# GLA values and gates of a head as seven block products, with weight block sums formed in DRAM by the DMA engines

## The chip, the cores and the metric

The kernel runs on one core of one Trainium2 chip. The metric is device time in microseconds (us) of one execution, from first to last instruction, and lower is better. TensorE (PE) multiplies matrices, VectorE (DVE) and ScalarE (ACT) do elementwise work, GpSimd (POOL) does small elementwise work and issues some of the DMAs, and SyncE (SP) issues most of the weight loads. Each engine takes its own instructions strictly in order; an instruction that waits for a semaphore holds up everything behind it on that engine.

## The reference

Two residual mixers on a sequence of 512 tokens of width 1024, then a final norm; all in float32.

```python
h = h + ssd_mixer(rmsnorm(h, ssd_norm), ...)     # 8 groups, 4 heads each, both directions
h = h + gla_mixer(rmsnorm(h, gla_norm), ...)     # 4 heads, both directions
return rmsnorm(h, final_norm)

def gla_mixer(u, w_in, w_gate, b_gate, onorm, w_out):
    q, k, v, z, gl = split(u @ w_in, ...)        # per head: q, k 128 wide, v, z 512 wide; gl 32 wide in all
    lg = log_sigmoid(gl @ w_gate + b_gate) / 16  # log gates, both directions
    o = gla_scan(q, k, v, lg_forward) + rev(gla_scan(reversed inputs))
    o = rmsnorm(o, onorm) * silu(z)
    return o @ w_out
```

The change touches `v` and `z` of the GLA half: for one head they are `u` (512 x 1024) times two weight blocks of 1024 x 512.

## The kernel before, in words

**Weights.** All weights pass through one ordered list (`W.add`, `W.next`). A piece is 128 x 1024 numbers (512 KB). SP loads it (L65) into one of three raw buffers; ACT casts it to `whi` (L85, or L90 with a scale) and DVE forms the rest `wlo` (L86 or L91), each in one of three buffers. A product of two float32 matrices is three matmuls (L137, L138, L139: high by high, high by low, low by high), since both factors are kept as a high and a low part. Two pieces are split ahead of the one that PE uses.

**SSD half.** For groups 0 to 7 PE makes projections (`proj_tok` into `ptk`, `proj_ch` into `pch`), and the scan of the group before is taken in steps between them. Once, in `dt_part`, the cumulative log decays `cum` are made (tile name `dy`); POOL writes them to DRAM in eight small DMAs (`cumd`, L390). Then, for every group, POOL loads two broadcast copies of them (`bct`, L492: 1 MB each), ACT adds a bias to `bct` (L570) and takes its exponential (L578), and PE uses it as weights (L611). The small norms of the SSD outputs (`rs`, L263 and L264) are on POOL too.

**GLA half.** After the last SSD output projection (`proj_out_rows`, tiles `pr`) the norm (`norm_T`, with PE transposes `ptn`, L281) fills `uh` and `ul`, the high and low part of the normed input, transposed. For each head come q and k (48 matmuls into `pch`), the output projection of the head before (96 matmuls into `po`), the gate `z` (`proj_tok`, 96 matmuls into `ptk`), attention (`bd`, `pta`, `pto`), and the next head's `v` (96 matmuls into `ptk`). The log gates `lgc` of all four heads are made once, before head 0 (L758 to L776).

**What sets the order.** The kernel is traced in the order of its code; a scheduler then orders each engine's instructions by priority and by when their inputs can be there. DMAs that POOL issues are instructions in POOL's own queue, and the scheduler may put one ahead of code that was written earlier if nothing that it reads is still to be written.

Of the kernel before, what the change touches and what calls it, by code (L numbers as in the profile page):

```python
# [18 lines left out]
NT = 4  # L19
# [96 lines left out]
def build(tc, I, out):  # L116
    nc = tc.nc
    ctx = ExitStack()
    with ctx:
# [28 lines left out]
        # ---- inputs and constants  # L148
# [5 lines left out]
        nbc2 = cp.tile([P, D], F32, name="nbc2")  # L154
# [30 lines left out]
        rmb = cp.tile([P, L], F32, name="rmb")  # L185
        nc.vector.memset(rmb, 1.0)
        nc.vector.memset(rmf.rearrange("p (c l) -> p c l", l=P)[:, :, 0:1], 0.0)
        nc.vector.memset(rmb.rearrange("p (c l) -> p c l", l=P)[:, :, P - 1 : P], 0.0)
# [54 lines left out]
        tokm(w_in2, GV0)  # L243
# [5 lines left out]
        for hd in range(GH):  # L249
            chan(w_in2, GQ0 + hd * P)  # L250
            chan(w_in2, GK0 + hd * P)
            if hd:
                outw(w_out2, (hd - 1) * 512, onT)
            tokm(w_in2, GZ0 + hd * 512)
            if hd + 1 < GH:
                tokm(w_in2, GV0 + (hd + 1) * 512)
# [9 lines left out]
        def norm_T(t, nb, xn):  # L266
# [8 lines left out]
            for hf in range(2):  # L275
# [8 lines left out]
                split(uh[sl], ul[sl], v)  # L284

# [57 lines left out]
        nc.sync.dma_start(nbc2, I["gla_norm"][0].partition_broadcast(P))  # L343
# [3 lines left out]
        # ================= SSD  # L347
        with tc.tile_pool(name="sp", bufs=1, reuse_waits="tile") as sp:
            TM = {}

            def dt_part():
# [17 lines left out]
                for c in (9, 7, 5, 3):  # L369
# [14 lines left out]
                    out=cum[32:64, ::-1], data0=rmb[32:64, ::-1], data1=la[32:64, ::-1], initial=0.0,  # L384
# [9 lines left out]
                # token-major copies  # L394
# [84 lines left out]
            def scan_group(g, bcx, zs):  # L479
# [20 lines left out]
                # token-major x and B  # L500
# [13 lines left out]
                # C B^T, [s, l] for every chunk  # L514
# [171 lines left out]
            for g in range(G + 1):  # L686
# [20 lines left out]
                for _ in it:  # L707
                    pass
            n2 = [nbc2[:, i * 512 : (i + 1) * 512] for i in range(2)]

            proj_out_rows(yts1(3), lambda t, hf: None)
# [4 lines left out]
        with tc.tile_pool(name="gp", bufs=1, reuse_waits="tile") as gp:  # L716
# [7 lines left out]
            for d in range(2):  # L724
                w = gp.tile([96, 512], F32R, tag="al", name=f"wgs{d}", bufs=4)
# [10 lines left out]
            def v_part(pts):  # L736
                vs = []
                for t in range(NT):
                    vh = gp.tile([P, 512], F32R, tag="vh", name="vh", bufs=5)
                    vl = gp.tile([P, 512], F32R, tag="vl", name="vl", bufs=5)  # L740
                    split(vh, vl, pts[t])
                    vs.append((vh, vl))
                return vs

            lgc = gp.tile([P, 8, L], F32, tag="big", name="lgc")

            def gates():
                pt = proj_ch(96)
                gl = gp.tile([96, L], F32R, tag="bds", name="gl")
                nc.scalar.copy(gl, pt[0:96])  # L750
                nc.vector.tensor_tensor(out=gl[64:96], in0=pt[64:96], in1=gl[64:96].bitcast(F32), op=ALU.subtract)
                ab = []
                for i in range(8):
                    d, hd = i // 4, i % 4
                    pt = wkb("ptg")
                    nc.tensor.matmul(pt, lhsT=wgs[d][:, hd * P : (hd + 1) * P], rhs=gl, start=True, stop=True)
                    a = gp.tile([P, L], F32, tag=f"sc{i}", name=f"ab{i}")
                    nc.scalar.activation(a, pt, AF.Abs, bias=bgT[:, i : i + 1])  # L758
                    nc.vector.tensor_scalar(
                        out=lgc[:, i], in0=pt, scalar1=bgT[:, i : i + 1], scalar2=0.0, op0=ALU.add, op1=ALU.min  # L760
# [3 lines left out]
                for i in range(8):  # L764
                    nc.scalar.activation(ab[i], ab[i], AF.Ln, bias=1.0)
                for i in range(8):
                    a = ab[i]
                    nc.vector.tensor_tensor(out=a, in0=lgc[:, i], in1=a, op=ALU.subtract)
                    if i < 4:
                        nc.vector.tensor_tensor_scan(  # L770
                            out=lgc[:, i], data0=rmf, data1=a, initial=0.0, op0=ALU.mult, op1=ALU.add
                        )
                    else:
                        nc.vector.tensor_tensor_scan(
                            out=lgc[:, i, ::-1], data0=rmb[:, ::-1], data1=a[:, ::-1], initial=0.0,
                            op0=ALU.mult, op1=ALU.add,  # L776
                        )
# [11 lines left out]
            def att_part(hd, q, k):  # L789
                res = []  # L790
                q4, k4 = b4(q), b4(k)
                for d in range(2):
                    cu = b4(lgc[:, d * 4 + hd])
# [17 lines left out]
                    # between blocks  # L811
# [26 lines left out]
                bds = gp.tile([P, 4, P], F32, tag="bds", name="bds")  # L838
# [70 lines left out]
            vs = v_part(proj_tok())  # L909
            gates()  # L910
            for hd in range(GH):
                q, k = qk_part(hd)
                att = att_part(hd, q, k)
                if hd:
                    proj_out(yts2(hd - 1))
                zs = z_gate(proj_tok(), gp, 2)
                o_part(hd, att, vs, zs)
                if hd + 1 < GH:
                    vs = v_part(proj_tok())
# [60 lines left out]
```

## Time and profile before

| | us |
|---|---|
| median of 3 runs | 896.43 (894.97 to 897.2) |
| profiled execution, span | 894.9 |
| PE busy | 861.4 |
| DVE busy | 604.6 |
| ACT busy | 469.4 |
| POOL busy | 59.9 |

The profiled execution has no time of its own besides its span, which is 1.5 us under the median and 0.1 us under the lowest run. Sums below are made against the span's rows and then added to the median. In the page's rows a line such as L86 is a line of the kernel before; `out<-in` are tile names, `xN` a count. Busy time of PE is the union of overlapping matmul records: a single record of 0.39 us overlaps with the next, which starts about 0.23 us after it.

### The profile page before, as it was taken

The page shows a single profiled execution, that of the slowest core. Times are in us where ns is not written, and L with a number is a line of the kernel's source. Part 1 is how long each engine was busy: PE and PEld are TensorE (multiplying, and loading weights), DVE is VectorE, ACT ScalarE, POOL GpSimd, SP SyncE. Part 2 cuts the span into 40 slices and gives each one's busy share as a digit, 9 for nine tenths or more (in the row PEclk, how much of TensorE's full clock was granted, in tenths as well). Part 3 has the DMA queues.
Part 4 walks back from the last instruction along what each step waited for, and adds up shares of the span by engine and source line. Part 5 has one row for each costly group of instructions (what it writes and reads, how often), then busy time and mean ns, then how long its engine had stood idle before and what let it go on. Part 6 is the DMA issues. An engine that isn't in the chain of part 4 may idle for free.

```text
span 894.9 us, 11133 instructions
## 1 busy us (share of the span) xinstructions
PE 861.4 (96%) x4072; PEld 705.4 (79%) x4072; DVE 604.6 (68%) x954; ACT 469.4 (52%) x1038; POOL 59.9 (7%) x135
## 2 busy tenths in 40 slices
PE   7999899999999999999989997999999999999996
PEld 5778778888888888887777776878887888788875
DVE  6399889997779977798877558646432663347353
ACT  6339487756576565764855474535232533243243
POOL 2011010001000000000002000000000000100012
PEclk9999999999999999999999998999999999999999
DMA  7334334224243342433221222123231323123202
GB/s 252 95 97 168 94 118 160 96 99 124 81 127 122 113 124 80 127 118 118 95 94 42 80 71 71 48 71 94 73 92 48 95 71 94 47 94 95 94 1 94
DMA packets 72789, 86.77 MB, mean 97 GB/s; under 512 B 7074, under 2 KB 48254, under 8 KB 70687
## 3 DMA queue, kind: packets, MB, share of 16 engines
q1 hardware_dynamic: 70028, 68.62, 25.6%
q0 software_dynamic: 2704, 17.44, 5.4%
q8 instruction: 32, 0.52, 0.2%
q14 instruction: 23, 0.18, 0.1%
q10 hardware_dynamic: 2, 0.00, 0.0%
HBM read 83.82 MB, written 2.23 MB: 96 GB/s over the span
## 4 chain that ended last, share of the span: by engine, by line
PE 44%; DVE 3%; ACT 3%; POOL 1%; issue 1%; POOLq 0%; ACTq 0%; DVEq 0%
PE ptk L138 6%; PE ptk L139 6%; PE ptk L137 6%; PE po L137 3%; PE po L138 3%; PE po L139 3%; PE pto L139 2%; PE pto L137 2%; PE pto L138 2%; PE pch L137 2%; PE pch L139 2%; PE pch L138 2%; PE pr L137 1%; PE pr L139 1%; PE pr L138 1%; PE pta L846 1%
## 5 line engine op out<-in xcount | busy, mean ns | idle before, releaser
L86 DVE TENSOR_TENSOR wlo<-wraw,whi 128x1024 fp32r<-128x1024 f32 (+1 forms) x90 | 109.1, 1213 | 122.6 <-ACT whi L85 122.4
L85 ACT CAST whi<-wraw 128x1024 fp32r<-128x1024 f32 (+1 forms) x90 | 93.7, 1042 | 172.2 <-PE ptk L139 90.5
L138 PE MATMUL ptk<-wlo,uh 128*128 128x512 f32 x384 | 153.1, 399 | 4.4 <-DVE wlo L86 4.4
L137 PE MATMUL ptk<-whi,uh 128*128 128x512 f32 x384 | 152.1, 398 | 0.9 <-ACT q L785 0.8
L139 PE MATMUL ptk<-whi,ul 128*128 128x512 f32 x384 | 152.4, 398 | 0.0
L138 PE MATMUL pch<-ul,whi 128*128 128x512 f32 (+2 forms) x336 | 133.4, 397 | 0.0
L137 PE MATMUL pch<-uh,whi 128*128 128x512 f32 (+2 forms) x336 | 133.2, 396 | 0.0
L139 PE MATMUL pch<-uh,wlo 128*128 128x512 f32 (+2 forms) x336 | 131.9, 393 | 0.0
L138 PEld LDWEIGHTS ptk<-wlo,uh 128*128 128x128 f32 x384 | 73.1, 190 | 19.7 <-DVE wlo L86 5.1
L137 PEld LDWEIGHTS ptk<-whi,uh 128*128 128x128 f32 x384 | 72.9, 190 | 16.3 <-ACT q L785 1.2
L139 PEld LDWEIGHTS ptk<-whi,ul 128*128 128x128 f32 x384 | 73.2, 191 | 15.0
L137 PEld LDWEIGHTS pch<-uh,whi 128*128 128x128 f32 (+2 forms) x336 | 62.5, 186 | 13.9
L138 PEld LDWEIGHTS pch<-ul,whi 128*128 128x128 f32 (+2 forms) x336 | 62.5, 186 | 13.7 <-issue 0.3
L139 PEld LDWEIGHTS pch<-uh,wlo 128*128 128x128 f32 (+2 forms) x336 | 62.5, 186 | 13.6
L447 DVE SCALAR_TENSOR_TENSOR cv<-pch,colA,cv 128x511 f32<-128x511 f32 (+1 forms) x96 | 70.7, 742 | 0.4
L90 ACT ACTIVATE whi<-wraw,colB 128x512 fp32r<-128x512 f32 x58 | 39.3, 717 | 49.1 <-PE pch L138 35.0
L91 DVE SCALAR_TENSOR_TENSOR wlo<-wraw,colB,whi 128x512 fp32r<-128x512 f32 x58 | 41.8, 748 | 30.9 <-ACT whi L90 30.6
L570 ACT ACTIVATE bct<-bct,eb 128x128 f32<-128x128 f32 x128 | 41.1, 393 | 21.1 <-DMA bct<-cumd 21.0
L578 ACT ACTIVATE bct<-bct,eb 128x128 f32<-128x128 f32 x128 | 41.2, 392 | 7.9 <-DVE bct L575 7.9
L139 PE MATMUL po<-whi,gyl 128*128 128x512 f32 x96 | 38.5, 401 | 0.0
L137 PE MATMUL po<-whi,yh 128*128 128x512 f32 x96 | 38.1, 400 | 0.3 <-DVE h L319 0.2
L139 PE MATMUL po<-whi,yl 128*128 128x512 f32 x96 | 38.1, 396 | 0.0
(252 smaller groups left out, 1542.3 us busy)
## 6 DMA issues: line engine op xcount, KB each, us to landing
wraw<-in_ssd_w_in_dram SPq DMA_DIRECT2D x48, 512.0 KB, 4.3
wraw<-in_gla_w_in_dram SPq DMA_DIRECT2D x40, 512.0 KB, 3.7
bct<-cumd POOLq DMA_DIRECT2D x16, 1024.0 KB, 5.2
wraw<-in_ssd_w_out_dram SPq DMA_DIRECT2D x16, 512.0 KB, 3.5
wraw<-in_gla_w_out_dram SPq DMA_DIRECT2D x16, 512.0 KB, 3.6
h<-in_x_dram SPq DMA_DIRECT2D x4, 512.0 KB, 5.4
out_dram<-o SPq DMA_DIRECT2D x8, 256.0 KB, 2.0
nbc<-in_gla_norm_dram SPq DMA_DIRECT2D x1, 512.0 KB
```

The lines of the kernel that those rows point to most:

```text
L85: nc.scalar.copy(vh, raw)
L86: nc.vector.tensor_tensor(out=vl, in0=raw, in1=vh.bitcast(F32), op=ALU.subtract)
L90: nc.scalar.mul(hs[j], raw[:, j], g)
L91: nc.vector.scalar_tensor_tensor(out=ls[j], in0=raw[:, j], scalar=g, in1=hs[j].bitcast(F32), op0=ALU.mult, op1=ALU.subtract)
L137: nc.tensor.matmul(pt, lhsT=a[0], rhs=b[0], start=first, stop=False)
L138: nc.tensor.matmul(pt, lhsT=a[0], rhs=b[1], start=False, stop=False)
L139: nc.tensor.matmul(pt, lhsT=a[1], rhs=b[0], start=False, stop=last)
L447: nc.vector.scalar_tensor_tensor(out=cv[:, o0:o1], in0=pt[:, o0 + s : o1 + s], scalar=cwt(j, a), in1=cv[:, o0:o1], op0=ALU.mult, op1=ALU.add,)
L570: nc.scalar.activation(bct[:, r], bct[:, r], AF.Identity, bias=TM["eb"][:, cc, i : i + 1])
L578: nc.scalar.activation(et[:, r], et[:, r], AF.Exp, bias=TM["eb"][:, cc, i : i + 1])
L846: mm = lambda a, bb, l, r: nc.tensor.matmul(pt[:, a * P : bb * P], lhsT=l, rhs=r, start=True, stop=True)
```

## The change

`v` and `z` of a head are one product of a 2 x 2 block matrix (the normed input, blocks a11 to a22 of 256 tokens by 512 inputs) with a 2 x 2 block matrix of weights (b11 and b21 for `v`, b12 and b22 for `z`, each 512 x 512). It was 8 block products (192 matmuls in all, 8 weight pieces); it is 7 (168 matmuls, 14 weight pieces of which each now serves 12 matmuls and not 24). Four of the seven take sums of weight blocks (w1 to w4). These are formed in DRAM, per head by four copies and four accumulating DMAs of 1 MB each, issued from POOL; the code asks for one of these 32 DMAs at each scan step of the SSD half from group 1 on. Four others take sums of input blocks (s2, s3, s4, q5), formed once on DVE and split on ACT and DVE. The results are put together by 14 DVE adds per head. The log gates are made per head, and `nbc2`, the row of GLA norm weights, is loaded at the start of the GLA half. The DMA descriptor space is cut from its default to 4096 bytes per partition.

```diff
-        for hd in range(GH):
+        class Blocks:
+            def __init__(self, hd):
+                v, z = GV0 + hd * 512, GZ0 + hd * 512
+                self.b11, self.b12 = w_in2[0:512, v : v + 512], w_in2[0:512, z : z + 512]
+                self.b21, self.b22 = w_in2[512:1024, v : v + 512], w_in2[512:1024, z : z + 512]
...
+            def step(self, n):
+                w = self.w
+                cp_, ad = (lambda d, s: nc.gpsimd.dma_start(d, s)), (
+                    lambda d, s: nc.gpsimd.dma_start(d, s, accum_op=ALU.add)
+                )
+                return (
+                    lambda: cp_(w["w1"], self.b11),
+                    lambda: cp_(w["w3"], self.b12),
+                    lambda: ad(w["w1"], self.b12),
+                    lambda: ad(w["w3"], self.b22),
+                    lambda: cp_(w["w2"], w["w1"]),
+                    lambda: ad(w["w2"], self.b22),
+                    lambda: cp_(w["w4"], w["w2"]),
+                    lambda: ad(w["w4"], self.b21),
+                )[n]()
...
+                for src in (self.b11, self.b21, w["w2"], w["w1"], w["w3"], w["w4"], self.b22):
+                    for kk in range(2):
+                        W.add(src[kk * 256 : (kk + 1) * 256].rearrange("(k p) f -> p k f", p=P), (2, 512))
+
+        blocks = [Blocks(hd) for hd in range(GH)]
+        sums = [(b, n) for n in range(8) for b in blocks]
...
                 def step():
+                    if g and sums:
+                        b, i = sums.pop(0)
+                        b.step(i)
                     n = -(-left[0] // max(left[1], 1))
...
+            nbc2 = gp.tile([P, D], F32, tag="lgc", name="nbc2")
+            nc.gpsimd.dma_start(nbc2, I["gla_norm"][0].partition_broadcast(P))
+            uf = [gp.tile([P, 4, L], F32, tag=tg, name=f"uf{tg}") for tg in ("gyh", "gyl")]
             for t in range(NT):
-                norm_T(t, n2, sp.tile([P, D], F32, tag="xt", name=f"xn2{t}", bufs=2))
+                norm_T(t, n2, gp.tile([P, D], F32, tag="zs", name=f"xn2{t}", bufs=2), uf)
...
+                two = range(2)
+                p1 = block_mm("a11")
+                m1 = [keep(i, "m1") for i in two]
+                for i in two:
+                    nc.scalar.copy(m1[i], p1[i])
+                p2 = block_mm("a12")
+                for i in two:
+                    split(*vs[i], add(tmp(), p2[i], m1[i]))
+                p6 = block_mm("s2")
+                u2 = [add(keep(i, "u2"), p6[i], m1[i]) for i in two]
+                p5 = block_mm("q5")
+                p7 = block_mm("s3")
+                u3 = [add(keep(i, "u3"), p7[i], u2[i]) for i in two]
+                for i in two:
+                    gate(2 + i, p5[i], u3[i])
+                for i in two:
+                    add(u2[i], p5[i], u2[i])
+                p4 = block_mm("a22")
+                for i in two:
+                    split(*vs[2 + i], add(tmp(), p4[i], u3[i]))
+                p3 = block_mm("s4")
+                for i in two:
+                    gate(i, p3[i], u2[i])
+                return vs, zs
...
-            vs = v_part(proj_tok())
-            gates()
+            gate_low()
+            qk = qk_part(0)
+            lgc = gates(0)
+            sums_of_u()
             for hd in range(GH):
-                q, k = qk_part(hd)
-                att = att_part(hd, q, k)
+                vs, zs = vz_part()
+                att = att_part(lgc, *qk)
                 if hd:
                     proj_out(yts2(hd - 1))
-                zs = z_gate(proj_tok(), gp, 2)
+                if hd + 1 < GH:
+                    qk = qk_part(hd + 1)
+                    lgc = gates(hd + 1)
                 o_part(hd, att, vs, zs)
...
-    nc = bacc.Bacc("TRN2", target_bir_lowering=False, num_devices=1)
+    nc = bacc.Bacc("TRN2", target_bir_lowering=False, num_devices=1, dynamic_dma_scratch_size=4096)
```

**Order on POOL, between the first norm and the first scan, before.** `n` and `nhalf` belong to the norm, `cumd` is the store of the log decays, `bct` the two broadcast loads of group 0; the names in brackets are the semaphores that an instruction waits for (DMASW0 to DMASW7: POOL's DMAs by turns).

```order
L274 TENSOR_TENSOR n_196<-n_196,nhalf 128x1 [waits Pool_49]
L390 DMA cumd<-dy 8x4x128 [waits DVE_49]
L390 DMA cumd<-dy 8x4x128
L390 DMA cumd<-dy 8x4x128 [waits DVE_49]
L390 DMA cumd<-dy 8x4x128 x5
L492 DMA bct<-cumd 128x2048 [waits DMASW2_49,DMASW3_49,DMASW1_49,DMASW0_49]
L492 DMA bct<-cumd 128x2048 [waits DMASW6_49,DMASW7_49,DMASW5_49,DMASW4_49]
```

The same place of the changed kernel; `wsumw` is a block of weight sums (L256 copies, L257 adds).

```order
L257 DMA wsumw_2_109<-in_gla_w_in_dram 512x512 [waits DMASW2_49]
L257 DMA wsumw_3_113<-in_gla_w_in_dram 512x512 [waits DMASW3_49]
L424 DMA cumd<-dy 8x4x128 [waits DVE_49]
L424 DMA cumd<-dy 8x4x128
L424 DMA cumd<-dy 8x4x128 [waits DVE_49]
L424 DMA cumd<-dy 8x4x128
L424 DMA cumd<-dy 8x4x128 [waits DMASW4_49]
L424 DMA cumd<-dy 8x4x128 [waits DMASW5_49]
L424 DMA cumd<-dy 8x4x128 [waits DMASW6_49]
L424 DMA cumd<-dy 8x4x128 [waits DMASW7_49]
L526 DMA bct<-cumd 128x2048 [waits DMASW2_49,DMASW3_49,DMASW1_49,DMASW0_49]
L526 DMA bct<-cumd 128x2048 [waits DMASW6_49,DMASW7_49,DMASW5_49,DMASW4_49]
```

All 32 DMAs of the weight sums have moved ahead of the `cumd` store: the first stands among POOL's set-up instructions, before the first norm, and the two adds shown here are the last. A DMA that reads a block or adds to it waits for the DMA that wrote the block, and the last four `cumd` stores wait for the last four adds.

**Order on ACT, where the first `bct` is used, before.** `whi` is a weight piece cast for PE, `cv` and `th` belong to the projections of group 1.

```order
L443 ACTIVATE cv_670<-pch,colB,colA 128x512 [waits PE_49]
L570 ACTIVATE bct<-bct,eb 128x128 [waits DMASW0_49]
L570 ACTIVATE bct<-bct,eb 128x128 x5
L513 COPY bt_696<-ptb 128x512 [waits PE_49]
L570 ACTIVATE bct<-bct,eb 128x128 x2
L570 ACTIVATE bct<-bct,eb 128x128 [waits DMASW1_49]
L85 CAST whi_851<-wraw_849 128x1024 [waits DMAHW4_49,PE_49]
```

And in the changed kernel:

```order
L477 ACTIVATE cv_681<-pch,colB,colA 128x512 [waits PE_49]
L604 ACTIVATE bct<-bct,eb 128x128 [waits DMASW0_49]
L604 ACTIVATE bct<-bct,eb 128x128 x5
L547 COPY bt_708<-ptb 128x512 [waits PE_49]
L604 ACTIVATE bct<-bct,eb 128x128 x2
L604 ACTIVATE bct<-bct,eb 128x128 [waits DMASW1_49]
L85 CAST whi_864<-wraw_862 128x1024 [waits DMAHW3_49,PE_49]
```

Nothing has moved here: the next weight piece is cast behind the first nine uses of `bct`, as before.

**Order on PE, at the end of the SSD half, before.** `ptk` is the first `v` projection, token block by token block; `ptn` the transposes of the norm.

```order
L138 MATMUL ptk_4415<-wlo_4170,uh 128x512
L281 MATMUL ptn<-idn,xn_4337 128x128 x4
L139 MATMUL ptk_4415<-whi_4169,ul 128x512
L281 MATMUL ptn<-idn,xn_4337 128x128 x4
L137 MATMUL ptk_4417<-whi_4163,uh 128x512
L281 MATMUL ptn<-idn,xn_4363 128x128 x4
L138 MATMUL ptk_4417<-wlo_4164,uh 128x512
```

And in the changed kernel, where `pr` is the last SSD output projection and `pch` the low-rank gate input:

```order
L137 MATMUL pr_4316<-xchw_4197,yh_3921 128x512
L138 MATMUL pr_4316<-bchw_4199,yh_3921 128x512
L139 MATMUL pr_4316<-xchw_4197,yl_3922 128x512
L314 MATMUL ptn<-idn,xn_4338 128x128 x8
L314 MATMUL ptn<-idn,xn_4366 128x128 x8
L314 MATMUL ptn<-idn,xn_4394 128x128 x8
L314 MATMUL ptn<-idn,xn_4422 128x128 x8
L137 MATMUL pch<-uh,whi_4208 96x512
```

The projections that stood between the transposes are gone from there: PE now goes through all four token blocks of the norm before the first product, which reads all 512 tokens at once.

## Rows read from the trace of the kernel before

**Rows 1.** The page's first part: busy time and share of the span, by engine.

```profile
PE 861.4 (96%) x4072; PEld 705.4 (79%) x4072; DVE 604.6 (68%) x954; ACT 469.4 (52%) x1038; POOL 59.9 (7%) x135
```

**Rows 2.** Timeline of POOL: start us, us, engine, line, op [idle before <-releaser].

```profile
64.31 4.67 POOL L390 DMA_DIRECT2D cumd<-dy  x8 [52.31 <-DVE dy L380]
68.98 0.59 POOL L492 DMA_DIRECT2D bct<-cumd  x1
70.75 0.57 POOL L492 DMA_DIRECT2D bct<-cumd  x1 [1.18 <-DMA cumd<-dy]
```

**Rows 3.** Timeline of ACT around the first use of bct.

```profile
75.75 1.87 ACT L570 ACTIVATE bct<-bct,eb 128x128 f32<-128x128 f32 x6 [0.23 <-DMA bct<-cumd]
...
79.30 1.05 ACT L85 CAST whi<-wraw 128x1024 fp32r<-128x1024 f32 x1
```

**Rows 4.** Busy time by stretch up to that use (DMA share, GB/s last).

```profile
0.00:22.40 22.40, 16.92 (x71) 12.04 (x72) 15.09 (x26) 14.03 (x32) 5.03 (x20) 1.00 0.74 252
22.40:44.80 22.40, 22.40 (x100) 17.21 (x99) 8.23 (x10) 8.46 (x12) 0.00 (x0) 1.00 0.35 95
44.80:67.20 22.40, 21.86 (x101) 17.48 (x100) 21.59 (x29) 8.48 (x12) 2.88 (x5) 1.00 0.35 97
67.20:75.80 8.60, 8.60 (x38) 6.62 (x37) 8.38 (x15) 7.44 (x16) 2.93 (x6) 1.00 0.72 263
```

**Rows 5.** DMA queues of the page: packets, MB, share of 16 engines' span.

```profile
q1 hardware_dynamic: 70028, 68.62, 25.6%
q0 software_dynamic: 2704, 17.44, 5.4%
...
HBM read 83.82 MB, written 2.23 MB: 96 GB/s over the span
```

**Rows 6.** DMA issues: count, KB each, median us to landing.

```profile
bct<-cumd POOLq DMA_DIRECT2D x16, 1024.0 KB, 5.2
```

**Rows 7.** Timeline of PE in the first GLA head: a wait and the matmuls around it.

```profile
542.78 0.39 PE L137 MATMUL ptk<-whi,uh 128*128 128x512 f32 x1
543.01 0.39 PE L138 MATMUL ptk<-wlo,uh 128*128 128x512 f32 x1
...
548.77 0.80 PE L138 MATMUL ptk<-wlo,uh 128*128 128x512 f32 x1 [4.24 <-DVE wlo L86]
549.37 0.63 PE L139 MATMUL ptk<-whi,ul 128*128 128x512 f32 x1
...
554.49 0.48 PE L138 MATMUL ptk<-wlo,uh 128*128 128x512 f32 x1
```

**Rows 8.** Timeline of PE at the end of the SSD half: last pr, transposes.

```profile
486.04 0.39 PE L139 MATMUL pr<-xchw,yl 128*128 128x512 f32 x1
...
491.48 0.63 PE L281 MATMUL ptn<-idn,xn 128*128 128x128 f32 x4 [0.73 <-DVE xn L276]
...
495.10 0.60 PE L281 MATMUL ptn<-idn,xn 128*128 128x128 f32 x4
```

**Rows 9.** Timeline of DVE there: the last part of the normed input.

```profile
496.35 0.69 DVE L143 TENSOR_TENSOR ul<-ptn,uh 128x512 fp32r<-128x512 f32 x1
```

**Rows 10.** Busy time in 90 us of the GLA half (columns as in Rows 4).

```profile
590.00:680.00 90.00, 89.25 (x412) 73.14 (x410) 43.29 (x64) 33.35 (x57) 2.96 (x8) 1.00 0.26 77
```

**Rows 11.** Groups of DVE by line, GLA half: count, busy us, mean ns.

```profile
L86 DVE TENSOR_TENSOR wlo<-wraw,whi 128x1024 fp32r<-128x1024 f32 x9 | 11.0, 1225 | 27.1 <-ACT whi L85 27.1
L91 DVE SCALAR_TENSOR_TENSOR wlo<-wraw,colB,whi 128x512 fp32r<-128x512 f32 x8 | 5.7, 749 | 6.2 <-ACT whi L90 6.2
L319 DVE TENSOR_TENSOR h<-h,po 128x512 f32<-128x512 f32 x8 | 5.2, 682 | 1.2 <-PE po L139 1.2
```

**Rows 12.** Groups of DVE by line, where the log gates are made.

```profile
L759 DVE TENSOR_SCALAR lgc<-ptg,colB 128x512 f32<-128x512 f32 x8 | 5.6, 746 | 2.9 <-ACT ab L758 2.9
L768 DVE TENSOR_TENSOR ab<-lgc,ab 128x512 f32<-128x512 f32 x8 | 5.1, 682 | 2.1 <-ACT ab L765 2.1
L770 DVE TENSOR_TENSOR_SCAN lgc<-rmf,ab 128x512 f32<-128x512 f32 x4 | 4.7, 1211 | 0.0
```

More of the change, by code (lines that the diff above doesn't have):

```diff
@@ L284, in norm_T @@
                 split(uh[sl], ul[sl], v)
+                if uf is not None:
+                    nc.scalar.copy(uf[hf][:, :, t * P : (t + 1) * P], v)
         def proj_ch(m=P):
@@ L712, in build, with blk @@
             for t in range(NT):
-                norm_T(t, n2, sp.tile([P, D], F32, tag="xt", name=f"xn2{t}", bufs=2))
-        with tc.tile_pool(name="gp", bufs=1, reuse_waits="tile") as gp:
+                norm_T(t, n2, gp.tile([P, D], F32, tag="zs", name=f"xn2{t}", bufs=2), uf)
+            f1, f2 = slice(0, 256), slice(256, 512)
+            a11, a12, a21, a22 = uf[0][:, :, f1], uf[1][:, :, f1], uf[0][:, :, f2], uf[1][:, :, f2]
+            def blk(n):
+                return [gp.tile([P, 4, 256], F32R, name=f"{n}{x}") for x in "hl"]
@@ new lines, in build, with sums_of_u, sub @@
+            SB = {n: blk(n) for n in ("q5", "s2", "s3", "s4")}
+            def sums_of_u():
+                def sub(out, neg, b):
+                    nc.vector.scalar_tensor_tensor(out=out, in0=neg, scalar=-1.0, in1=b, op0=ALU.mult, op1=ALU.subtract)
+                x, y = (gp.tile([P, 4, 256], F32, tag="zs", name=f"t{n}", bufs=2) for n in ("x", "y"))
+                nc.vector.tensor_tensor(out=x, in0=a22, in1=a21, op=ALU.subtract)
+                sub(y, x, a11)
+                split(*SB["s2"], y)
+                split(*SB["q5"], x)
+                nc.vector.tensor_tensor(out=x, in0=a11, in1=a21, op=ALU.subtract)
+                split(*SB["s3"], x)
+                sub(y, y, a12)
+                split(*SB["s4"], y)
@@ new lines, in build, with block_mm @@
+            UB = {
+                "a11": (uh[:, 0:4, f1], ul[:, 0:4, f1]),
+                "a12": (uh[:, 4:8, f1], ul[:, 4:8, f1]),
+                "a22": (uh[:, 4:8, f2], ul[:, 4:8, f2]),
+                **SB,
+            }
+            def block_mm(name):
+                pts = [mmb(f"pb{i}") for i in range(2)]
+                bh, bl = UB[name]
+                for kk in range(2):
+                    wh, wl = W.next()
+                    for i in range(2):
+                        sl = slice(i * P, (i + 1) * P)
+                        for j in range(2):
+                            k = 2 * kk + j
+                            mm3(pts[i], (bh[:, k, sl], bl[:, k, sl]), (wh[j], wl[j]), k == 0, k == 3)
+                return pts
@@ L763, in gates @@
                     ab.append(a)
[L764 to L777, printed above, removed]
+                for a in ab:
+                    nc.scalar.activation(a, a, AF.Ln, bias=1.0)
+                for d, a in enumerate(ab):
+                    nc.vector.tensor_tensor(out=a, in0=lgc[:, d], in1=a, op=ALU.subtract)
+                    lv, av = (lgc[:, d], a) if d == 0 else (lgc[:, d, ::-1], a[:, ::-1])
+                    nc.vector.tensor_tensor_scan(
+                        out=lv, data0=rmf, data1=av, initial=0.0, op0=ALU.mult, op1=ALU.add
+                    )
+                return lgc
             def b4(t):
@@ L956, in build @@
                 W.alt[len(W.specs) - 1] = lambda: [
-                    [gp.tile([P, 512], F32R, tag=tg, name=f"{tg}w{j}", bufs=5) for j in range(2)] for tg in ("vh", "vl")
+                    [gp.tile([P, 512], F32R, tag=tg, name=f"{tg}w{j}", bufs=4) for j in range(2)] for tg in ("vh", "vl")
                 ]
```

82 lines of the change are left out of this document (46 added, 36 removed).

## The prediction

> **What bounds the kernel now.** I read the page's busy times first: PE is busy 861 of 895 us, DVE 605, POOL 60 [rows 1]. So PE's time is what counts, and a change pays if it takes matmuls from PE and lets no other engine make PE wait. Full-speed matmuls start 0.23 us apart [rows 7], and that is PE's price for one. Then I read the timelines where the order of the changed kernel differs, because POOL, nearly idle, is where new instructions went. The reader should see two things there. POOL stores the log decays at 64.31 us, as soon as DVE has them, and issues the first two broadcast loads at 68.98 and 70.75 us [rows 2]. ACT takes up the first of them at 75.75 us, having waited for that DMA, and casts the next weight piece for PE at 79.30 us, behind it in its queue [rows 3]. So there is a chain: POOL's queue, then `bct`, then ACT's queue, then PE's weights.
>
> **The change part by part.**
>
> *Matmuls.* 24 of 192 go per head, 96 in all: 96 x 0.23 = 22 us off PE [rows 7]. This is the whole gain.
>
> *The 32 weight-sum DMAs.* They stand in POOL's queue ahead of the `cumd` stores and so ahead of every `bct` load. POOL is in order, and the sums depend on each other, so POOL sits in front of the last adds until the earlier sums have landed. The last four `cumd` stores wait for the very last adds. So the first scan begins only when all 32 MB have been formed. Until then ACT stands at its first `bct`, the cast behind it is not made, and PE runs out of weights about 10 us later. The sum needs t, the time when the last add has landed.
>
> Price of a copy (1.05 MB from DRAM to DRAM): the trace has no such transfer; it wrote 2.23 MB in all [rows 5]. The SP queue took 25.6% of 16 engines' 894.9 us for 68.62 MB, so with all 16 engines at work 3.34 us per MB or 3.5 us for a block; POOL's queue took 5.4% for 17.44 MB, 2.9 us for a block [rows 5]. A 1 MB `bct` load lands 5.2 us after its issue [rows 6], which is the price of a lone one with its latency. Ends: 2.9 and 5.2. I take 4.4, midway between 3.5 (rows of the same kind, 2 KB and shorter pieces) and 5.2, since the destination has to be written in DRAM too. It cannot be free, because no stretch moves more than 263 GB/s [rows 4].
>
> The page "DMA: Bandwidth & Descriptors" of the Trainium skill, section "Latency and other measured facts", gives 207 to 214 GB/s for copies within DRAM in pieces of 16 KiB; no row here shows one. By it a block would take 5.0 us (an estimate), and with adds at twice that the sums would take 240 us and the kernel about 1094 us.
>
> Price of an add: the destination is read as well, so two reads for one write. Ends: the cheapest copy (2.9, the second read wholly hidden) and three passes of the dearest (15.6). I take twice the copy, 8.8. The page "Collectives: The Full Stack" of the Trainium skill, section "The bandwidth ceiling: the fold count and why AG ≠ RS ≠ AR", says that an add in the DMA engines costs its second source read and not the arithmetic; it measured a ratio of 1.93, and no row here shows it. By it the sums would take 206 us and the kernel 1061 us.
>
> Sum: 16 copies x 4.4 + 16 adds x 8.8 = 211 us of all engines. Beside them run the loads of the first 75.8 us: 0.74 x 22.4 + 0.35 x 22.4 + 0.35 x 22.4 + 0.72 x 8.6 = 38 us of all engines [rows 4], less 6 for two `bct` loads, which in the new order come later: 32 to 33. POOL issues the first copy at about 1 us. So t = 1 + 33 + 211 = 245 us.
>
> From t to the first use of `bct`: one `cumd` issue (4.67 / 8 = 0.6 us) and then the same way as before, from 68.98 to 75.75, 6.8 us [rows 2, 3]. ACT's first `bct` moves from 75.75 to 252, by 177 us. Before, the next weight piece was ready at 79.30 + 1.05 + 1.22 = 81.6 [rows 3, 11] while PE still had one of 24 matmuls (5.5 us) in hand; I take 2 us of that as slack that is used up first: 175 us. Whatever the sums do to the first 75 us (x and weights land later, POOL's small norm instructions stand between DMA issues) lies inside this wait and costs nothing, as long as it is under 170 us.
>
> After a long wait PE starts slowly. The one long wait in the trace (4.24 us) is followed by 13 matmuls in the 5.7 us from 548.77 to 554.49, about 0.43 us apart, the lower of the two clock levels, where 13 x 0.23 = 3.0 would do: 2.7 us [rows 7]. I add it once.
>
> *The norm before the GLA half.* Before, PE did projections between the transposes; now it does all transposes first and then a product that needs all tokens. From the end of the last `pr` (486.43) to the end of the last `ul` (497.04) are 10.6 us [rows 8, 9]; of these the 26 transposes left there take 3.7 (at most 0.16 us each, four in 0.63), and PE has nothing else to do now: 7 us. `nbc2`, loaded late, waits for scan work that ends before the last projection, so its landing (5.2 us for twice the bytes [rows 6]) is hidden by that projection; if it were not, up to 5 us more.
>
> *Product stage.* The fifth product's two PSUM banks are held until the sixth (s3) and two adds are done, and the next product (a22) takes the banks of s3 after the first add: 0.68 us [rows 11] and the handing over, about 1 us, and the product after it waits on a similar add. I take 1.5 us per head, 6 in all; ends 0 and 4 x 4.2 = 17, the long wait of [rows 7] once per head.
>
> *DVE and ACT.* Per head DVE gets 6 more splits (7.4 us), 14 adds (9.5) and, for heads 1 to 3, its gates (2 x (0.75 + 0.68 + 1.21) = 5.3) [rows 11, 12]: 22 us on top of 43 in 90 [rows 10], so 65 in about 85. ACT has 33 in 90 [rows 10] and gets less than that. Both stay under PE on the mean, so I cost them at nothing; what hides them is PE's own matmuls. Within the product stage it is tight: 168 x 0.23 = 39 us of PE against 14 x 1.23 + 14 x 0.68 + 4 x 0.69 + 4 x 0.75 = 32 us of DVE without attention's share. That is a rival.
>
> *The rest* (one memset fewer, descriptor space, tile places): nothing, a few tenths either way.
>
> Sum: 175 + 3 - 22 + 7 + 6 = +169. Against the span 894.9 + 169 = 1064; on the median of the runs 1065 us.
>
> **The rivals.**
> 1. *DVE sets the pace in the product stage.* For it: 32 of 39 us of DVE there before attention's instructions come in, and each piece now lasts PE 12 matmuls, 2.8 us, and not 5.5. Against: two pieces are split ahead. Price: a wait with its slow stretch as in [rows 7], 4.24 + 2.7 = 6.9 us, once per head, 28 us: 1093 us.
> 2. *The sums are cheap.* If a second read costs nothing and a copy 2.9 us, they take 32 x 2.9 = 93, t = 127, and the kernel 1065 - 118 = 947 us. For it: POOL's queue did move a block in that much engine time [rows 5]. Against: those loads do not write DRAM.
> 3. *The adds are dear.* Copies at 5.2 and adds at 15.6: 333 us, t = 367, 1187 us. For it: nothing in the trace adds in a DMA. Against: the arithmetic alone has no row that makes it slow.
> 4. *The other side: faster.* If the sums had landed when `cum` is ready at 64.31 us [rows 2], POOL's queue would hold up nothing, and the change would give -22 + 7 + 6: 887 us. It decides at t = 64: 32 x 1.05 = 33.6 MB within 63 us beside the loads, 533 GB/s, counted once; the fastest stretch moves 263 [rows 4]. A later t costs t - 70, so it would be faster up to t = 76 and within 0.3% up to 82.
>
> That the change does not do what it says is part of the forecast: the sums do not run during the SSD half, they run before its first scan.
>
> **How the numbers follow.** Forecast 0.60 (985 to 1130 us: the sums between 131 and 276 us, GLA as summed); rival 1 0.15; rival 2 0.10; rival 3 0.12; rival 4 0.03, of which 0.02 faster and 0.01 no change. I predict 1065 us. The range takes in the forecast and rival 1 and part of the way to rivals 2 and 3: 985 to 1165, about 0.78. A difference of 0.3%, 2.7 us, is about what a measurement of this kernel can tell from none. Faster 0.02, the same 0.01, slower 0.97.
>
> **What would show it right or wrong.** In the profile of the changed kernel, PE's busy tenths should fall to nothing in the slices from about 90 us to about 250 us, the DMA row be high from the start until then, ACT's longest wait be for `bct` and end where the last `cumd` store has landed, and PE's matmul records be 96 fewer with a busy total about 20 us lower. POOL should be seen waiting for its own DMAs. After the gap the SSD half should take as long as before. It is wrong if the first `bct` is used near 76 us (POOL not blocked), if PE idles in the GLA half for more than some 20 us, or if PE is fed in spite of the blocked scan.

## The result, and the profile of the changed kernel

The changed kernel takes 981.95 us (median of 4 runs, 977.90 to 985.65) against 896.82 for the kernel before (4 runs): ratio 1.0949, 95% interval 1.0914 to 1.0984, so it is slower by 85 us. The prediction said 1065 with a range of 985 to 1165. The sign and the place of the loss were right; the time lies 83 us under the forecast and just below the range.

The page of the changed kernel: busy times, then PE's row, clock and DMA row in 40 slices, and the queues.

```profile
span 983.9 us, 11252 instructions
...
PE 859.3 (87%) x3976; PEld 699.9 (71%) x3976; DVE 674.3 (69%) x1040; ACT 513.4 (52%) x1088; POOL 90.1 (9%) x168
...
PE   3937226889999999999998987999999999999997
...
PEclk9968558999999999999999997999999999999999
DMA  9999999235324243243423410362353244316302
...
q1 hardware_dynamic: 76412, 80.68, 27.8%
q0 software_dynamic: 13728, 51.52, 19.2%
...
HBM read 129.96 MB, written 35.78 MB: 168 GB/s over the span
```

PE has 96 matmuls fewer than in [rows 1], yet it is hardly less busy, since the granted clock fell in the first 170 us, to 5 tenths in two slices (1.2 GHz, the lower of its two levels), where it had stood waiting for weights. The hole is at the front: PE is at 3 tenths from 49 to 74 us and at 2 from 98 to 148 us (a slice is 24.6 us), with the DMA row full until some 165 us. From there on PE's row is at 8 or 9 almost throughout.

POOL's timeline (start us, us; in brackets the idle time before and what ended it), to lay beside [rows 2]:

```profile
114.32 0.52 POOL L256 DMA_DIRECT2D wsumw<-wsumw  x1 [4.70 <-DMA wsumw<-in_gla_w_in_dram]
120.55 0.49 POOL L256 DMA_DIRECT2D wsumw<-wsumw  x1 [5.71 <-DMA wsumw<-in_gla_w_in_dram]
126.79 0.49 POOL L256 DMA_DIRECT2D wsumw<-wsumw  x1 [5.76 <-DMA wsumw<-in_gla_w_in_dram]
130.11 1.05 POOL L257 DMA_DIRECT2D wsumw<-in_gla_w_in_dram  x1 [2.83 <-DMA wsumw<-wsumw]
133.17 1.02 POOL L257 DMA_DIRECT2D wsumw<-in_gla_w_in_dram  x1 [2.00 <-DMA wsumw<-wsumw]
136.15 1.00 POOL L257 DMA_DIRECT2D wsumw<-in_gla_w_in_dram  x1 [1.96 <-DMA wsumw<-wsumw]
...
150.39 3.48 POOL L424 DMA_DIRECT2D cumd<-dy  x6 [3.73 <-DVE dy L414]
158.11 0.54 POOL L424 DMA_DIRECT2D cumd<-dy  x1 [4.25 <-DMA wsumw<-in_gla_w_in_dram]
164.57 0.55 POOL L424 DMA_DIRECT2D cumd<-dy  x1 [5.92 <-DMA wsumw<-in_gla_w_in_dram]
165.56 0.58 POOL L526 DMA_DIRECT2D bct<-cumd  x1 [0.45 <-DMA cumd<-dy]
```

These rows give both prices. The copies of the w4 chain are released one by one as the adds before them land, 6.2 us apart; the adds after them as the copies land, 3.0 us apart. So, with the weight loads running beside them, an add costs 6.2 us and a copy 3.0. The last `cumd` store waits until 164.57 for the last add: that is t, predicted as 245. But look at 150.39: POOL had nothing left to issue before that store and waited 3.73 us for DVE to deliver the decays themselves (`dy`), which were ready at 64.31 in [rows 2].

ACT's first use of `bct`, which answers to [rows 3], and what ACT waited for in the first 171 us (total, times, longest):

```profile
170.72 1.87 ACT L604 ACTIVATE bct<-bct,eb 128x128 f32<-128x128 f32 x6 [2.26 <-DMA bct<-cumd]
```

```profile
ACT whi L85 <- DMA wraw<-in_ssd_w_in_dram: 117.0, 13, 21.4
ACT uh L142 <- PE ptn L314: 6.2, 3, 4.6
ACT xn L303 <- DMA h<-in_x_dram: 5.6, 3, 2.0
ACT bct L604 <- DMA bct<-cumd: 2.3, 1, 2.3
```

ACT hardly stood at `bct`. In all it stood 117 us waiting for weight pieces that had not come. The span grew by 89.0 us: 95.0 before the first `bct` (75.75 to 170.72), and 6.0 were won after it.

Why the weights were late, in a stretch that is all sums and weights (30 to 72 us; queue: packets, MB, share of 16 engines):

```profile
DMA packets 6917, 9.69 MB, mean 231 GB/s; under 512 B 1332, under 2 KB 3320, under 8 KB 6916
...
q0 software_dynamic: 3458, 7.85, 88.8%
q1 hardware_dynamic: 3458, 1.82, 21.0%
```

Both queues moved exactly 3458 packets. POOL's are 2.3 KB on average, those of the channel weights on SP's queue 0.53 KB, so the weights got 1.82 MB where [rows 4] show 95 GB/s (4.0 MB in 42 us). The page "DMA: Bandwidth & Descriptors" of the Trainium skill, section "Queues, rings and completion order", says that an engine takes its queues in turn, one packet at a time. These equal counts agree, if the profile's packet is the page's, which no run here shows; the experiments test the turns.

### The profile page after: what moved, and what is told of

Its sections match the earlier page's. It is cut to its first block, busy times and chain, and to the rows that moved or that the text cites. A ratio compares the mean times of both kernels' runs of the same rounds, so it can differ in the third digit from the quotient of the medians.

```text
span 983.9 us, 11252 instructions
## 1 busy us (share of the span) xinstructions
PE 859.3 (87%) x3976; PEld 699.9 (71%) x3976; DVE 674.3 (69%) x1040; ACT 513.4 (52%) x1088; POOL 90.1 (9%) x168
## 5 line engine op out<-in xcount | busy, mean ns | idle before, releaser
L86 DVE TENSOR_TENSOR wlo<-wraw,whi 128x1024 fp32r<-128x1024 f32 (+1 forms) x114 | 138.4, 1215 | 162.5 <-ACT whi L85 162.4
L85 ACT CAST whi<-wraw 128x1024 fp32r<-128x1024 f32 (+1 forms) x114 | 118.8, 1042 | 240.4 <-DMA wraw<-in_ssd_w_in_dram 117.0
L137 PE MATMUL pch<-uh,whi 128*128 128x512 f32 (+2 forms) x336 | 139.1, 415 | 38.7 <-ACT whi L85 18.8
L137 PE MATMUL ptk<-whi,uh 128*128 128x512 f32 x128 | 52.4, 409 | 9.1 <-ACT uh L142 9.1
L139 PE MATMUL ptk<-whi,ul 128*128 128x512 f32 x128 | 52.0, 406 | 0.0
L138 PE MATMUL ptk<-wlo,uh 128*128 128x512 f32 x128 | 51.5, 402 | 0.0
L296 POOL TENSOR_SCALAR rs<-ss 128x2 f32<-128x2 f32 (+1 forms) x32 | 8.3, 260 | 424.8 <-ACT gy L1010 322.7
L137 PE MATMUL pb<-whi,uh 128*128 128x512 f32 x96 | 37.8, 394 | 1.2 <-ACT whi L85 1.2
L138 PE MATMUL po<-wlo,yh 128*128 128x512 f32 x96 | 38.3, 399 | 0.0
L138 PE MATMUL pb<-wlo,uh 128*128 128x512 f32 x96 | 38.0, 395 | 0.0
```

What stands on the lines that cost most here:

```text
L85: nc.scalar.copy(vh, raw)
L86: nc.vector.tensor_tensor(out=vl, in0=raw, in1=vh.bitcast(F32), op=ALU.subtract)
L137: nc.tensor.matmul(pt, lhsT=a[0], rhs=b[0], start=first, stop=False)
L138: nc.tensor.matmul(pt, lhsT=a[0], rhs=b[1], start=False, stop=False)
L139: nc.tensor.matmul(pt, lhsT=a[1], rhs=b[0], start=False, stop=last)
L296: nc.gpsimd.tensor_scalar(out=dst, in0=ss, scalar1=mul, scalar2=add, op0=ALU.mult, op1=ALU.add)
```

## The experiments

Theory when they began: the loss lies wholly at the front and comes from the sums' transfers, which starve the weight loads there; POOL's blocked queue adds little. Rivals: the blocked queue alone; the product stage; bytes wherever they go. The table's times are medians; "SSD end" is the start of the SSD half's last `pr` matmul in the one profiled run, "rest" the span after it, so a difference of a few us in these two columns may be that run's alone (e9's six runs spread over 4.5 us). Of the kernel before they are 486.0 and 408.9 us, of the changed kernel 587.4 and 396.5.

| run | us | ratio to before (95%) | SSD end | rest |
|---|---|---|---|---|
| e1_spread | 934.48 | 1.0424 (1.0385 to 1.0464) | 533.2 | 393.7 |
| e2_nosum | 883.30 | 0.9840 (0.9815 to 0.9864) | 486.4 | 396.3 |
| e3_copies | 962.84 | 1.0725 (1.0691 to 1.0759) | 567.7 | 396.3 |
| e4_cumsp | 980.44 | 1.0916 (1.0889 to 1.0942) | 582.7 | 396.4 |
| e5_strips | 994.20 | 1.1086 (1.1034 to 1.1137) | 599.1 | 395.4 |
| e6_spread_sp | 897.63 | 1.0015 (0.9994 to 1.0037) | 498.6 | 395.2 |
| e7_late | 911.01 | 1.0156 (1.0129 to 1.0183) | 489.5 | 420.2 |
| e8_start | 904.12 | 1.0098 (1.0063 to 1.0133) | 490.2 | 412.1 |
| e9_even | 886.01 | 0.9866 (0.9836 to 0.9896) | 496.8 | 391.2 |
| e10_even1k | 887.32 | 0.9886 (0.9861 to 0.9912) | 495.1 | 390.9 |
| e11_best | 887.72 | 0.9888 (0.9864 to 0.9912) | 495.0 | 390.9 |
| e12_free | 897.96 | 1.0017 (1.0000 to 1.0035) | 507.2 | 390.6 |

**e2_nosum: what the change is worth without its sums.**

```
-    for src in (self.b11, self.b21, w["w2"], w["w1"], w["w3"], w["w4"], self.b22):
+    for src in (self.b11, self.b21, self.b22, self.b12, self.b12, self.b21, self.b22):
-sums = [(b, n) for n in range(8) for b in blocks]
+sums = []
```

> Leaves the 32 sum transfers out; the products that should read w1 to w4 read plain blocks of the weight in their place, so it is the time of everything but the sums. Theory (the sums' transfers are the whole loss): 882 to 892, middle 887, first bct near 76 us. Rival A (the product stage costs the time): 970 to 985. Rival C (the norm at the boundary, which now takes 17 us from the last output product to the first GLA product where it took 10.6, eats the gain): 893 to 900.

883.30 us. The product stage does pay: the rest of the span after the SSD half is 12.6 us shorter than before, and the SSD half as long as before. Rivals A and C fall.

**e4_cumsp: free POOL's queue, leave the sums.**

```
-    nc.gpsimd.dma_start(cumd[...], cum[...])
+    nc.sync.dma_start(cumd[...], cum[...])
-    nc.gpsimd.dma_start(bct..., TM["cumd"]...)
+    (nc.sync if g < 2 else nc.gpsimd).dma_start(bct..., TM["cumd"]...)
```

> The cumd stores and the bct loads of groups 0 and 1 are issued by SP in place of POOL, so nothing that the first scans need stands behind the sums on POOL; the sums' transfers stay as they are. Theory (weight loads starved beside the sums make cum itself late, at 150 us, so the queue adds only what lies from there to 165.6): total 955 to 975, middle 967. Rival E (the blocked queue is the loss, as the prediction had it, and the first 75 us are free): first bct near 80 to 90 us, total 895 to 910.

980.44 us: nothing won, where the predicted mechanism should have given everything back, so rival E falls. The decays are as late as in the changed kernel (the second scan that makes them starts at 150.37 us, 150.12 there). It also missed the theory's 955 to 975: the stores took SP 13 us to issue, so the `bct` loads went out at 167.22, no earlier than POOL's 165.56.

```profile
153.74 13.24 SPq L424 DMA_DIRECT2D cumd<-dy  x8
167.22 1.33 SPq L526 DMA_DIRECT2D bct<-cumd  x2
```

**e3_copies: cheap adds.** The adds become plain copies.

```
-    lambda d, s: nc.gpsimd.dma_start(d, s, accum_op=ALU.add)
+    lambda d, s: nc.gpsimd.dma_start(d, s)
```

> The 16 accumulating transfers become plain copies of the same bytes in the same places of POOL's queue (the block sums are then wrong). Theory (transfer time sets t, a copy of 1 MB takes 3.0 us and an add 6.2): t falls from 164.6 to some 16 x 3.2 = 51 us less, 113, total 925 to 940, middle 931. Rival D (the order on POOL and the waits of the adds for their copies set t, not the price of an add): 965 to 985.

962.84 us, outside the ranges of both theory and rival, but it teaches: the last sum was issued at 114.12 us, near the expected 113, but the decays came only at 144.7 us, so the saving was 19 us and not 51. POOL had issued all its sums 30 us before, and its first `cumd` store waited for DVE alone:

```profile
144.94 1.79 POOL L424 DMA_DIRECT2D cumd<-dy  x3 [30.20 <-DVE dy L414]
```

In 30 to 72 us the sums' packets are now 4.7 KB, and the weights got still less, 1.46 MB in almost exactly as many packets as the sums:

```profile
q0 software_dynamic: 2761, 13.04, 91.8%
q1 hardware_dynamic: 2764, 1.46, 13.1%
```

Faster sums starve the weights harder while they last. This run shows the starved weights as a cause by themselves: with no sum left for POOL to issue, the SSD half still ends 81 us after that of e2.

**e5_strips: shorter packets for the sums.** On top of e4:

```
+    def strips(d, s, **kw):
+        for c in range(0, 512, 128):
+            nc.gpsimd.dma_start(d[:, c : c + 128], s[:, c : c + 128], **kw)
-    cp_, ad = (lambda d, s: nc.gpsimd.dma_start(d, s)), (...)
+    cp_, ad = strips, lambda d, s: strips(d, s, accum_op=ALU.add)
```

> As e4 (the first scans need nothing from POOL's queue), but each sum goes in four strips of 128 columns, so that its packets are 512 B as those of the channel weights, at the same total of bytes. Theory F (the two busy queues take turns packet by packet, so the small packets of the weights lose against packets four times as long): in 30 to 72 us q1 moves more than twice its 1.82 MB, the cumd stores go out before 120 us in place of 150, and the total falls to 930 to 960. Rival G (what is shared is the bytes that the memory gives, whatever the packets): q1 gets no more than 2 MB there, cumd at 150 us or later, total 975 or more, since 512 B packets are no cheaper for the sums.

The mechanism came out as theory F has it, the total did not. In 30 to 72 us:

```profile
q0 software_dynamic: 6838, 6.66, 81.3%
q1 hardware_dynamic: 7895, 4.04, 35.9%
```

The weights get 4.04 MB, as much as without sums (4.09 in e1, which has none there yet), and the decays are ready at 71.5 us. The sums' packets came out at 0.97 KB on average, not 512 B. The sums moved 15% less than before in that time, far too little to explain 2.2 times the weights; so packet length decides the sharing. But the total rose to 994.20 us, because now the other cover lies bare (a cover is here a wait that hides another one of like length): the small root of each group's norm stands on POOL behind the sums, and ACT waits for it. In strips the sums also hold POOL longer: the last one was issued at 216.06 us, against 145.63 in the changed kernel.

```profile
218.15 0.91 ACT L664 ACTIVATE y<-y,rs 128x256 f32<-128x256 f32 x2 [97.84 <-POOL rs L299]
```

**e12_free: both covers gone, sums still at the front.** On top of e5:

```
-    (nc.sync if g < 2 else nc.gpsimd).dma_start(bct...)
+    nc.sync.dma_start(bct...)
-    nc.gpsimd.tensor_scalar(out=dst, ...); nc.gpsimd.tensor_tensor(out=dst, ..., op=ALU.pow)
+    nc.vector.tensor_scalar(out=dst, ...); nc.vector.tensor_tensor(out=dst, ..., op=ALU.mult)
```

> As e5 (sums at the front in strips with 512 B packets, cumd on SP), but nothing of the SSD half is left behind them on POOL: all bct loads are on SP, and the small root of each group's norm runs on VectorE, as a product in place of the power, so the norm's values are not the reference's. e5 had cum at 70 us and then lost 98 us where y waited for that root behind the sums. Theory (two covers, each as dear by itself: starved weight loads, and POOL's blocked queue; only with both gone does the front cost little): 895 to 925, the sums done near 200 us and no single wait over 15 us. Rival J (sums at the front cost their transfer time in any case): 960 or more.

897.96 us, 96 less than e5, with the same bytes moved from the first us on. The last sum was issued at 238.05, later than the 200 expected. Rival J falls: the SSD half ends 21 us after that of e2, not 100. (The roots of the GLA heads moved to VectorE too, and no kernel without sums was run in that form, so the 21 us are not exact.) So most of the loss is not the transfers but what waits for them, either in the DMA engines or in POOL's queue, and each of the two alone makes most or all of it: the starved weights 81 us in e3, the blocked queue 113 us in e5, where the strips hold it longer.

**e1_spread: the sums really in the SSD half.** POOL keeps the written order there:

```
+    with tc.manual_schedule(engines={mybir.EngineType.Pool}):
         for g in range(G + 1):
```

> The same 32 block-sum transfers, but POOL keeps the written order in the SSD loop: the first copy stands behind the cumd stores, the sums stand one by one between the bct loads of groups 0 to 5, and no sum is issued in the first 75 us. Theory (the whole loss lies at the front, where the sums starve the weight loads and hold cumd and bct): the first bct is used near 76 us as in the kernel before, the product stage keeps its gain of some 6 us, total 885 to 900, middle 891. Rival A (the product stage itself, with more VectorE work and waits, costs the time wherever the sums stand): 970 to 985. Rival B (33.5 MB of sums beside the SSD half's weights slow it wherever they stand, the first bct early but the scans late): 915 to 960, with ACT and PE waits for wraw spread over 75 to 400 us.

934.48 us. The first `bct` is back at 79.7 us, but rival B's 915 to 960 holds: the SSD half ends 47 us after that of e2, and what is waited for is `bct`, not weights as rival B had it:

```profile
ACT bct L604 <- DMA bct<-cumd: 50.2, 8, 17.6
```

In e2 ACT waits 21.3 us for `bct` and in the kernel before 21.0, so 29 us of these are new; and now they reach PE, which waits 27.9 us for the copies to `xt` that stand behind them on ACT (none in e2). A `bct` load now lands 10.6 us after its issue, where [rows 6] have 5.2.

**e6_spread_sp: the same, `bct` loads on SP's queue.**

```
-    nc.gpsimd.dma_start(bct..., TM["cumd"]...)
+    nc.sync.dma_start(bct..., TM["cumd"]...)
```

> As e1 (the sums behind the cumd stores, spread over groups 0 to 5), but the bct loads are issued by SP, so that they don't wait in the software queue behind the sums. In e1 ACT waited 50.2 us for bct. Theory H (the 43 us that e1 lacks to the 883 of the kernel without sums are bct loads standing behind sums in one queue): 885 to 900, ACT's wait for bct below 15 us. Rival I (the sums beside the other transfers slow each load whatever its queue): 915 to 935.

897.63 us, ACT's wait for `bct` 13.5 us, a landing 5.1 us. Theory H holds: in POOL's queue a load waits behind the sums issued before it; in SP's it does not. This wins 37 us. It does not win everything: the SSD half still ends 12 us after that of e2, and ACT now waits 15.0 us for weight pieces there.

**e7_late and e8_start.** e7 issues the sums of heads 2 and 3 in the GLA half; e8 also takes head 0's first two products ahead of the projections.

```
+    if hd and hd + 1 < GH:
+        for n in range(8):
+            blocks[hd + 1].step(n)
     vs, zs = vz_part()
```

> As e6, but only the sums of heads 0 and 1 (16 transfers) go in the SSD half, two for each group; those of heads 2 and 3 go at the start of heads 1 and 2 of the GLA half, POOL in written order there too. Theory H and I both: less than or the same as e6; by H 884 to 895 (the sums cost nothing once no load stands behind them), by I about half of e6's excess over 883 is gone.

911.01 us: both expectations wrong. The SSD half gets better by 9 us, but the GLA half loses 25 us against e6. There ACT waits 33.0 us for weight pieces made by the sums (1.8 in e6) and PE 13.1 us for an add on DVE:

```profile
ACT whi L85 <- DMA wraw<-wsumw: 33.0, 11, 5.3
```

These loads were not late for want of their sums. In 600 to 635 us they fetch head 1's sums, the last of which was issued at about 433 us, while head 2's are being formed; yet half of them land 10.6 us or more after their issue (count, KB each, median us to landing), where e6 has 3.5 in the same stretch:

```profile
wraw<-wsumw SPq DMA_DIRECT2D x5, 512.0 KB, 10.6
```

The two queues again move nearly equal counts there, 1837 packets of the sums and 1904 of SP's loads. So the loads are late because they share the engines with the next head's sums.

```
+    vz = vz_parts(); next(vz)        # products a11, a12 of head 0
     gate_low()
     qk = qk_part(0)
```

> As e7, and the first two products of head 0 (a11, a12: token tiles 0 and 1 alone) go ahead of the gate, query and key projections, to fill TensorE's waits at the norm between the halves, where e2 waits 9.6 us for xn. If those waits are what the norm costs: 4 to 9 us less than e7; if the products only take the place of the projections that wait for tiles 2 and 3 anyway: the same as e7 within 2 us.

904.12 us, 6.9 less than e7, as the first expectation had it; the rest after the SSD half is 8 us shorter. Between e6 and e11 below, which also differ in this start, the rest shrinks by only 4.3 us, so 8 is not what it gives everywhere. The norm between the halves is a real cost: in the changed kernel PE's last output product starts at 587.42 us and its first GLA matmul at 604.82, with two long waits for `xn` in between. They can be filled in part.

```profile
587.42 0.39 PE L139 MATMUL pr<-xchw,yl 128*128 128x512 f32 x1
591.98 2.81 PE L314 MATMUL ptn<-idn,xn 128*128 128x128 f32 x12 [4.17 <-DVE xn L309]
...
599.72 1.94 PE L314 MATMUL ptn<-idn,xn 128*128 128x128 f32 x8 [3.36 <-DVE xn L309]
...
604.82 1.59 PE L137 MATMUL pch<-uh,whi 128*96 128x512 f32 x3
```

**e9_even, e10_even1k, e11_best: all together.** Sums four to a group, `bct` on SP, e8's start; e10 in strips of 256 columns; e11 with the sum that e9 and e10 lack.

```
-    if g and sums:
+    if g and sums and len(sums) > 32 - 4 * g:             # e9, e10
+    if g and sums and len(sums) > max(31 - 4 * g, 0):     # e11
-    cp_, ad = (lambda d, s: nc.gpsimd.dma_start(d, s)), (...)
+    cp_, ad = strips, lambda d, s: strips(d, s, accum_op=ALU.add)   # e10: as e5, step 256
```

> All 32 sums in the SSD half again, behind the cumd stores, but evenly: four for each of the eight groups (e6 has them done by group 5), bct on SP as in e6, and the start of the GLA half as in e8. Split by halves of the profiled runs: e6's SSD half ended 12 us later than that of the kernel without sums (last output product 498.6 against 486.4), e7's with half the sums spread evenly 3 us later; the GLA half takes 396 us in e2 and 395 in e6, and e8 had 8 us less than e7 there. Theory (what is left of the cost is the density of the sums beside the loads): SSD half to 490 to 495, GLA half 388, total 880 to 889. Rival (the cost goes with the bytes, not with their density): SSD half to 498, total 889 to 894.

> As e9, but each sum goes in two strips of 256 columns, so its packets are half as long. If turns by packet still cost the weight loads anything when the sums are spread: SSD half 2 to 5 us shorter than e9's. If the shorter packets only make the sums themselves longer: the same as e9 within 2 us, or up to 5 us longer.

> e9 with all 32 sums issued before the loop ends (e9's last group had three steps for its four sums, so the last sum of head 3 was missing there, and a part of its output was wrong): the sums run five in group 1, four in groups 2 to 7, three in the last. Theory: the one add more, 6.2 us of transfer among others at the loop's start, changes nothing that the path sees: 884 to 890, the fastest of the kernels with sums. Rival: the last sums now stand later against head 0's first loads of w2 and w4 and hold the GLA half: 890 to 896.

e9 took 886.01 us, within the theory's total, but its SSD half (496.8) came out between theory and rival, and its rest (391.2) missed the 388. By the profiled runs even spreading won 1.8 us of e6's 12 in e9 and 3.6 in e11. The profiled run of e9 is the slowest of its six and that of e6 lies 2.1 us under its median, so the 1.8 is rather too low. e10 is within 1.3 us of e9, so where the sums are spread, packet length no longer shows. e11, complete, takes 887.72 us, within its theory: 1.1% faster than the kernel before, the only kernel here with all its sums and all its work that beats both. Its page:

```profile
span 885.9 us, 11259 instructions
...
PE 843.0 (95%) x3976; PEld 691.5 (78%) x3976; DVE 673.5 (76%) x1040; ACT 515.7 (58%) x1090; POOL 79.9 (9%) x152
...
PE   7998999999999999999979799989999999999996
```

Against e2 the SSD half still pays 8.6 us (495.0 - 486.4) for the sums. No experiment split that. Nor does any run have the default descriptor space: in the changed kernel POOL waits 61.3 us between the adds for nothing that the profile shows, and whether the smaller space has to do with it was not tested.

## Why the prediction was wrong

It was right that the scheduler's order decides: the sums run before the first scan, and that costs far more than the product stage gives. Two steps under that failed.

*The price of the sums (the step "Sum: 16 copies x 4.4 + 16 adds x 8.8 = 211 us").* Measured: 16 x 3.0 + 16 x 6.2 = 147 us, 64 us less. The ratio, twice a copy, was right (6.2 / 3.0 = 2.07). The copy was wrong: 3.0 us is close to the low bound of 2.9 that POOL's own rows gave, and I had moved away from it by averaging with 5.2, a time to landing. In the queue one copy is done 3.0 us after another; a latency prices one transfer, not a queue of them. What is left of t for the loads beside is 16 us (164.6 - 1 - 147) and not 33. That is a remainder and not a measurement: in the first 165 us POOL's queue has 83.7% of the engines' time, 138 us, and SP's 22.3%, 37 us, so in part the two lie over each other, and adding them, as the sum did, counts some time twice. Together these shift t by -80 us, which is the miss: first `bct` at 170.7, predicted 252. With the measured t the prediction's path gives 172, but that this comes out is luck: the starved weights, which the path does not have, ended at nearly the same time.

*"Whatever the sums do to the first 75 us lies inside this wait and costs nothing."* False as a mechanism. I let the weight loads run at their old pace beside the sums and charged only the sums. In fact they got 1.82 MB where 4 were needed, and the decays came at 150. POOL's queue then held their last store only 14 us longer (150.39 to 164.57), and most of that was hidden too, since ACT, late from its weights, came to `bct` only at 168.5 us and waited 2.3 us there. The blocked queue still ends last, but by these 2.3 us. It would have cost as much alone, as e5 shows in a longer form; in this kernel the starved weights cost nearly the same by themselves (e3). e4, which was to take the queue away, can't show what it is worth, since SP issued the loads just as late. The sign that I gave for it, ACT's longest wait at `bct`, was absent: 2.3 us against 117.0 in all for weights. Nor did PE's busy time fall by some 20 us; it fell by 2.1, because PE did the work of the starved stretch at the lower clock.

The smaller terms. After the first `bct` the sum gave about -8 us, measured -6.0. The matmuls, the norm and the bank waits together were -22 + 7 + 6 = -9; the rest after the SSD half shrank by 12.4. Within it the norm's 7 fits (PE waits 9.6 us at the transposes after the SSD half, 1.1 in the kernel before), and the bank waits' 6 were too many: from the last output product of the SSD half on, PE's only wait at one of the seven products is this (total, times, longest):

```profile
PE pb L137 <- ACT whi L85: 1.2, 1, 1.2
```

For the slow clock after the wait the sum had 2.7 us. The stretch from the first `bct` to the SSD end took 416.7 us against 410.4 in e2, 6.3 more, with a granted clock of 0.94 from 170 to 230 us; what part of the 6.3 is the clock was not separated.

*The rivals.* DVE does not set the pace in the product stage: it is busy 63 of 90 us, up from 43 in [rows 10] and near the 65 of 85 computed, and PE is busy as before (columns as in [rows 4]):

```profile
690.00:780.00 90.00, 88.45 (x407) 72.85 (x406) 63.24 (x91) 46.70 (x74) 4.32 (x8) 1.00 0.39 117
```

Cheap sums (947) had the copy's price right and the add's wrong. Dear adds did not occur. Faster did not come at this place of the sums, even with both covers gone (e12, ratio 1.0017). It came in the order that the code was written in, with `bct` in another queue, the sums spread evenly and head 0's first products moved forward (e11); with only the first two of these the time is that of the kernel before (e6, 1.0015). The bound of 263 GB/s on which I leaned against it was low: the changed kernel moves 338 GB/s in its first 30 us.

## What to carry to other kernels

Price a queue of transfers by engine time per byte, and then ask what else the same DMA engines must deliver meanwhile: in these runs, while both had work waiting, the queue with short packets got bytes only in the ratio of the packet lengths. When work is moved to the front of a queue, list everything that waits for it by two roads, in the queue and in the shared engine; with two waits of the same length that cover each other, taking away one shows almost nothing. What the source says on the place of an instruction without dependences is not where it runs: look at the order, and pin it.

## What the runs showed of the hardware that I had not expected

- Two busy queues share the DMA engines packet for packet: 3458 and 3458 in the changed kernel, 2761 and 2764 in e3, with bytes as the packet lengths have it (7.85 to 1.82 MB, 13.04 to 1.46).
- A copy of 1.05 MB from DRAM to DRAM takes 3.0 us in a queue of such copies, an accumulating one 6.2, both beside the weight loads (changed kernel).
- A 1 MB load issued behind the sums in their queue lands in 10.6 us (e1), in SP's queue beside them in 5.1 (e6); without sums it is 5.2 (e2).
